# A decoder layer on one core: the value half of the last compressed sequence moves from the 256-key query tile to the last one

## The chip, the cores and the metric

The kernel runs on one core of a Trainium2 chip. The metric is the device time of one execution in microseconds (us); less is better. Each number under "time" is a median of several runs of the same kernel. TensorE is called PE, VectorE DVE, ScalarE ACT, GpSimd POOL and SyncE SP; SP only issues transfers here.

## The reference

One step of a hybrid decoder layer is computed for two groups that share the weights: a prompt of 1024 tokens, and 8 sample sequences of 8 new tokens each behind 2048 past ones. The layer is a half feed-forward block, a combined projection, attention and a Mamba-2 mixer side by side, the projection w_out, and a second half feed-forward block. Every attention has a compressed branch. For the sample group its keys and values come from the cache: overlapping blocks of 32 past tokens go through a small two-layer network, for keys (K) and for values (V) with weights of their own.

```python
def compress(rows, pe, w1, w2):
    ...
    blk = jnp.concatenate([ch[:, :-1], ch[:, 1:]], axis=2) + pe[None, None, :, None, :]
    blk = blk.transpose(0, 1, 3, 2, 4).reshape(b, nc - 1, KV_HEADS, CMP_BLOCK * HEAD_DIM)
    return jax.nn.silu(blk @ w1) @ w2

def nsa_mixer(q, q_pos, full_cmp, full_sel, o_win, gates, prm, slopes, sel_qb):
    kc = compress(full_cmp[:, :, 0], prm['cmp_pe_k'], prm['cmp_w1_k'], prm['cmp_w2_k'])
    vc = compress(full_cmp[:, :, 1], prm['cmp_pe_v'], prm['cmp_w1_v'], prm['cmp_w2_v'])
    o_cmp, p_cmp = cmp_attention(q, q_pos, kc, vc, slopes)
    idx = select_blocks(p_cmp, q_pos, n_sel_blocks)
    o_sel = sel_attention(q, q_pos, idx, full_sel[:, :, 0], full_sel[:, :, 1], slopes, sel_qb)
    return g[:, :, 0] * o_cmp + g[:, :, 1] * o_sel + g[:, :, 2] * o_win
```

The kernel returns the outputs of both groups and their new cache rows and states.

## The kernel before

The program is one long list of instructions in which a scheduler fixes the order on each engine when the kernel is built, after the dependencies and the order in which the code emits them. Matrix products in float32 are made of three matmuls on a high and a low part (names that end in h and l, or hi and lo).

**Prompt attention.** A loop runs over eight query tiles of 128 queries, in the order `KN["qt"] = (2, 7, 6, 5, 4, 3, 1, 0)`. Tile 1, the seventh, sees 256 keys; tile 0, the eighth and last, sees 128. For each tile and head PE computes scores `s` (lines 1808, 1810, 1813), VectorE their maximum `mx` (1818), ScalarE the exponentials `pb` (1824), which are scaled by the row sums; PE transposes them (`pT`, 1846) and multiplies by the values (`o`, 1855). The eight exponentials of each of the two branches make 16 per tile.

**Compression of the samples.** It is emitted as work beside the query tiles: the list `KN["cs"]` says how many of the eight sequences are emitted ahead of each tile. `compress_sample(b)` gathers the cached rows `chk` of one sequence (POOL, 1689), and does the K half and then the V half. A half has four steps `pairs(kv, jj)`: two copies `chp` (267), four transposes `cT` on PE (1712), and the split into `th` (ScalarE) and `tl` (VectorE, 1717). Each step feeds 12 matmuls `cA` with the weights `w1h` and `w1l` (1733 to 1735). Behind four steps come the hidden layer `cxh` (1410 to 1414), two matmuls `c` (1740 for K, 1743 for V), and the copy to `kcTs` or `vcs`. `pairs` runs one step ahead of its matmuls, over the border from K to V too. The last sequence, number 7, is emitted ahead of the 256-key tile.

**What comes next.** After the query tiles the space of the compression (the weights `w1h` among it) is given up, and `sample_attention()` uses it. It loads `big` (SP, 1951), a table of constants, masks and selector rows; the window rows `schk` (SP, 2052); the rows of the selected blocks, `schk` as well, by gathers on POOL (2048). SP also brings rows `xT` (1892) and pieces `raw` of w_out (1900). PE transposes the rows (`kT_ps`, 2064), computes gates (`a_ps<-gates,big`, 1985) and scores of the compressed keys (`a_ps<-kcTs,QS`, 1994), from which a chain of short instructions on VectorE and ScalarE (1987 to 2004, ending in `pcg`) makes the probabilities that choose the blocks (2006 onward). The matmuls `wout` (250 to 252) of the projection fill PE between the parts of that stage.

Of the kernel before, what the change touches and what calls it, by code (L numbers as in the profile page):

```python
# [18 lines left out]
P = 128  # L19
# [15 lines left out]
PAST = 2048  # L35
AHEAD = 5
EARLY = {(0, 0): (0, 128), (1, 0): (640,), (0, 1): (), (1, 1): (768,)}
KN = {'Bt': 'a', 'cb': 'a', 'de': 'vv', 'ea': 'pp', 'st': 'p', 'hT': 'v', 'xm': 'p', 'yz': 'v', 'kT': 'aa', 'sPT': 'v', 'ce': 'v', 'cm': 'v', 'pcT': 'v', 'msk': 'a', 'osb': 'av', 'q': 'sspss', 'pb': ['apppaapp', 'apppappp', 'apppappp', 'apvpappp', 'apppapvp', 'appvappp', 'vpvvvpvv', 'pvvvvvvv'], 'pc': 'p', 'ob': 'aa', 'QA': 'aapv', 'QB': 'pv', 'chp': 'ap', 'th': 'aa', 'qt': (2, 7, 6, 5, 4, 3, 1, 0), 'cs': [3, 0, 2, 1, 1, 0, 1, 0]}
SLOPES = [2.0 ** -(h + 1) for h in range(NH)]


# [39 lines left out]
def hybrid_step(ctx: ExitStack, tc: tile.TileContext, *aps):  # L81
    nc = tc.nc
# [1591 lines left out]
    with pool("att", bufs=2) as K, pool("att_ps2", bufs=3, space=PSUM) as PS2, \  # L1674
# [27 lines left out]
        def compress_sample(b):  # L1702
            chk = gather(b) if b else first_chk
            def pairs(kv, jj):
                chp = CK.tile([P, 2, 2, 2, 64], F32, name="chp", bufs=1)
                for g in range(2):
                    copy(KN["chp"][g], chp[:, :, g], chk[:, 4 * jj:4 * jj + 4, kv, g, :].rearrange(
                        "p (j r) d -> p j r d", r=2))
                q = b1("cT")
                for u in range(2):  # L1710
                    for g in range(2):
                        nc.tensor.transpose(q[:, P * (2 * u + g):P * (2 * u + g) + P],
                                            chp[:, u, g].rearrange("p r d -> p (r d)"), ident)
                sv = q.rearrange("p (u c) -> p u c", u=2)
                th, tl = tpad[jj % 2]
                copy(KN["th"][jj % 2], th[:, :, :256], sv)
                nc.vector.tensor_tensor(tl[:, :, :256], sv, f32(th[:, :, :256]), op=OP.subtract)

            steps = [(kv, jj) for kv in range(2) for jj in range(4)]
            pairs(*steps[0])  # L1720
            for kv in range(2):
                ab = PSC.tile([P, 2, P], F32, name="cA")
                for jj in range(4):
                    if (kv, jj) != steps[-1]:
                        pairs(*steps[4 * kv + jj + 1])
                    th, tl = tpad[jj % 2]
                    for u in range(2):
                        j = 2 * jj + u
                        for z in range(2):
                            wh, wl = w1h[:, kv, 8 * z + j], w1l[:, kv, 8 * z + j]  # L1730
                            first = j == 0 and z == 0
                            mh, ml = (x[:, u, z:z + 256].rearrange("p (g c) -> p g c", g=2) for x in (th, tl))
                            nc.tensor.matmul(ab, wh, mh, start=first, stop=False, skip_group_check=True)  # L1733
                            nc.tensor.matmul(ab, wl, mh, start=False, stop=False, skip_group_check=True)
                            nc.tensor.matmul(ab, wh, ml, start=False, stop=(j == 7 and z == 1), skip_group_check=True)
                hs = cmp_hidden(CK, ab[:, :, :127], None, kv, 127)
                q = b1("c2")
                for g in range(2):
                    if kv == 0:
                        nc.tensor.matmul(q[64 * g:64 * g + 64, :127], w2[:, 0], hs[:, g, :127],  # L1740
                                         start=True, stop=True)
                    else:
                        nc.tensor.matmul(q[:127, 64 * g:64 * g + 64], hs[:, g, :127], w2[:, 1],
                                         start=True, stop=True)
                if kv == 0:
                    nc.vector.tensor_copy(kcTs[:, b, :127], q[:, :127])
                else:
                    nc.vector.tensor_copy(vcs[:127, b, :], q[:127, :P])

        sequences = iter(range(8))  # L1750
        for qi, qt in enumerate(KN["qt"]):
            tq = slice(P * qt, P * qt + P)
            for _ in range(KN["cs"][qi]):
                compress_sample(next(sequences))
            QBq = QBs[2 * (qi % 2):2 * (qi % 2) + 2]
            lo_, up_ = slice(0, 64), slice(64, 128)
            QAs = QA0
# [27 lines left out]
            for g in range(2):  # L1785
                PT = {}
                for br in range(2):
# [6 lines left out]
                    for hh_ in range(4):  # L1794
# [26 lines left out]
                                nc.vector.tensor_reduce(mx[:, 1 + i:2 + i], parts[i][0], axis=AX.X, op=OP.max)  # L1821
                            nc.vector.tensor_reduce(mx[:, 0:1], mx[:, 1:3], axis=AX.X, op=OP.max, negate=True)  # L1822
                        for i, (s, st, pn) in enumerate(parts):
                            nc.scalar.activation(pb[:, st:st + pn], s, AF.Exp, bias=mx[:, 0:1],  # L1824
                                                 accum_out=part[:, hh_, i:i + 1])
                    total = part[:, :, 0]
                    if ns == 2:
                        total = sm[:, 1 + br, hs_]
# [35 lines left out]
                copy(KN["ob"][1], ob[up_], Ov[up_, :, 1])  # L1864
                nc.vector.tensor_tensor(qT[lo_, 2 * g:2 * g + 2, tq], Ov[lo_, :, 0], ob[lo_], op=OP.add)
                nc.vector.tensor_tensor(qT[up_, 2 * g:2 * g + 2, tq], Ov[lo_, :, 1], ob[up_], op=OP.add)
    Ds.close()
    KVs.close()

# [663 lines left out]
```

## Time and profile before

| | before |
|---|---|
| median of 3 runs | 2470.27 us (2468.21 to 2471.36) |
| the profiled execution, own time | 2475.45 us |
| its span, first to last instruction | 2473.8 us |
| its mean granted PE clock | 0.987 |
| PE busy | 2408.8 us, 97% |
| DVE, ACT, POOL busy | 1744.7, 1131.2, 418.3 us |

A stretch's busy time on an engine is the time in which the engine worked on an instruction. The granted clock is a share of the full 2.4 GHz. The times of rows count from the first instruction of the profiled execution.

### The profile page before, as it was taken

What the parts mean: (1) busy time and instruction counts of PE and PEld (TensorE: products, weight loads), DVE (VectorE), ACT (ScalarE), POOL (GpSimd) and SP (SyncE); (2) the same over time, 40 slices, a digit from 0 to 9 for tenths busy, and PEclk for the clock granted to TensorE, in tenths of its full rate; (3) what the DMA queues carried; (4) which work ended last, traced back from release to release, by engine and by line L of the source; (5) the groups of instructions that cost most, each with busy time, mean ns of one, the idle gap of its engine ahead of it and who ended that gap; (6) DMA issues with size and microseconds to landing.
All of it is one profiled execution on the core that took longest, in us unless ns stands there. A gap on an engine that the chain in (4) does not pass through costs nothing.

```text
span 2473.8 us, 48193 instructions
## 1 busy us (share of the span) xinstructions
PE 2408.8 (97%) x19026; PEld 2222.8 (90%) x19026; DVE 1744.7 (71%) x3673; ACT 1131.2 (46%) x2501; POOL 418.3 (17%) x533
## 2 busy tenths in 40 slices
PE   7999999999999999999999999999999999999998
PEld 6999999999999998997667766677899999999998
DVE  6777776677778855655656666777967676768776
ACT  7544444441133254425666675444545454543113
POOL 0000000011134343333434343111000000001110
PEclk9999999999999999999999998999999999999999
DMA  4334343598652333423110104476235353559654
GB/s 162 134 133 160 130 164 129 175 338 306 230 190 84 126 116 102 119 69 127 40 64 35 69 35 148 130 250 213 89 123 171 120 174 120 174 213 370 238 209 153
DMA packets 230446, 379.07 MB, mean 153 GB/s; under 512 B 18509, under 2 KB 147705, under 8 KB 228812
## 3 DMA queue, kind: packets, MB, share of 16 engines
q1 hardware_dynamic: 210248, 318.02, 37.7%
q0 software_dynamic: 7600, 38.59, 4.5%
q10 hardware_dynamic: 12372, 19.38, 2.2%
q8 instruction: 150, 2.46, 0.4%
q14 instruction: 76, 0.62, 0.1%
HBM read 255.66 MB, written 124.40 MB: 154 GB/s over the span
## 4 chain that ended last, share of the span: by engine, by line
PE 86%; DVE 6%; DMA 4%; ACT 3%; issue 1%; POOL 0%; ACTq 0%; DVEq 0%; POOLq 0%
PE dq L634 6%; PE gY L367 6%; PE dq L633 6%; PE dq L635 6%; PE gY L368 6%; PE gY L366 6%; PE gX L367 5%; PE gX L366 5%; PE gX L368 5%; PE o L1855 3%; PE pT L1846 3%; PE s L1808 1%; PE xbc L250 1%; PE xbc L251 1%; PE xbc L252 1%; PE cA L1733 1%
## 5 line engine op out<-in xcount | busy, mean ns | idle before, releaser
L634 PE MATMUL dq<-db,da 128*128 128x256 f32 (+1 forms) x1232 | 353.2, 288 | 0.3 <-DVE da L270 0.3
L635 PE MATMUL dq<-db,da 128*128 128x256 f32 (+1 forms) x1232 | 352.8, 288 | 0.0
L633 PE MATMUL dq<-db,da 128*128 128x256 f32 (+1 forms) x1232 | 349.8, 288 | 2.7 <-DVE Cc L386 2.2
L642 DVE TENSOR_TENSOR xT<-xT,dq 128x256 f32<-128x256 f32 (+1 forms) x456 | 186.9, 432 | 84.8 <-PE dq L635 83.2
L270 POOL TENSOR_TENSOR ds<-dw 128x512 f32<-128x512 f32 x22 | 29.5, 1341 | 1228.1 <-DVE wlo L270 508.0
L633 PEld LDWEIGHTS dq<-db,da 128*128 128x128 f32 x1232 | 230.5, 189 | 3.3 <-DVE Cc L386 2.5
L635 PEld LDWEIGHTS dq<-db,da 128*128 128x128 f32 x1232 | 232.8, 189 | 0.0
L634 PEld LDWEIGHTS dq<-db,da 128*128 128x128 f32 x1232 | 231.9, 188 | 0.6 <-DVE da L270 0.5
L267 ACT CAST whi<-ws 128x512 fp32r<-128x512 f32 x156 | 96.5, 623 | 205.9 <-PE gY L368 137.6
L270 DVE TENSOR_TENSOR wlo<-raw,whi 128x512 fp32r<-128x512 f32 x184 | 125.5, 687 | 83.9 <-ACT whi L267 83.5
L267 ACT CAST da<-ds 128x512 fp32r<-128x512 f32 x88 | 52.6, 623 | 234.7 <-PE dq L635 93.4
L267 ACT CAST whi<-raw 128x512 fp32r<-128x512 f32 x181 | 112.4, 626 | 72.0 <-PE g L414 19.5
L270 DVE TENSOR_TENSOR wlo<-ws,whi 128x512 fp32r<-128x512 f32 x156 | 106.7, 687 | 42.4 <-ACT whi L267 41.9
L1824 ACT ACTIVATE pb<-s,mx 128x256 f32<-128x256 f32 (+3 forms) x192 | 105.0, 552 | 59.7 <-DVE mx L1822 37.6
L1846 PEld LDWEIGHTS pT<-ident,pb 128*128 128x128 f32 x528 | 59.6, 143 | 45.8 <-issue 40.1
L1821 DVE TENSOR_REDUCE mx<-s 128x1 f32<-128x384 f32 (+2 forms) x128 | 66.6, 536 | 44.0 <-PE s L1813 34.1
L366 PE MATMUL gY<-B3h,whi 128*128 128x256 f32 (+1 forms) x320 | 91.5, 287 | 1.5 <-ACT whi L267 1.4
L366 PE MATMUL gX<-B6h,whi 128*128 128x256 f32 (+1 forms) x320 | 91.3, 286 | 0.9 <-ACT Cc L373 0.9
L367 PE MATMUL gX<-B6h,wlo 128*128 128x256 f32 (+1 forms) x320 | 91.4, 286 | 0.6 <-DVE wlo L270 0.6
L367 PE MATMUL gY<-B3h,wlo 128*128 128x256 f32 (+1 forms) x320 | 91.6, 287 | 0.2 <-DVE wlo L270 0.2
L277 POOL TENSOR_TENSOR pb<-pb,sm 128x640 f32<-128x640 f32 (+7 forms) x70 | 85.1, 1238 | 37.6 <-DVE sm L1831 34.0
L367 PE MATMUL gY<-B2h,wlo 128*128 128x256 f32 (+1 forms) x320 | 91.4, 286 | 0.0
(763 smaller groups left out, 8548.1 us busy)
## 6 DMA issues: line engine op xcount, KB each, us to landing
db<-GD SPq DMA_DIRECT2D x42, 1632.0 KB
GD<-Cc SPq DMA_DIRECT2D x154, 272.0 KB
GD<-his SPq DMA_DIRECT2D x84, 272.0 KB
raw<-in_ffn_wu_dram SPq DMA_DIRECT2D x22, 1024.0 KB
dw<-in_ffn_wd_dram SPq DMA_DIRECT2D x44, 512.0 KB
raw<-in_ffn_wg_dram SPq DMA_DIRECT2D x21, 1024.0 KB
GD<-hp SPq DMA_DIRECT2D x70, 272.0 KB
db<-GD SPq DMA_DIRECT2D x14, 1088.0 KB
```

Source lines behind the costliest of these rows:

```text
L267: return nc.scalar.copy(out, src) if eng == "a" else ENGINES[eng].tensor_copy(out, src)
L270: ENGINES[eng].tensor_tensor(out, x, y, op=op)
L277: nc.gpsimd.tensor_tensor(out, x, by.to_broadcast(list(x.shape)), op=OP.mult)
L366: nc.tensor.matmul(q, ah[:, k], b_, start=first, stop=False, skip_group_check=True)
L367: nc.tensor.matmul(q, al[:, k], b_, start=False, stop=False, skip_group_check=True)
L368: nc.tensor.matmul(q, ah[:, k], c_, start=False, stop=(k == 3), skip_group_check=True)
L633: nc.tensor.matmul(q, x, bh[:, u, o], start=first, stop=False, skip_group_check=True)
L634: nc.tensor.matmul(q, y, bh[:, u, o], start=False, stop=False, skip_group_check=True)
L635: nc.tensor.matmul(q, x, bl[:, u, o], start=False, stop=(u == np_ - 1), skip_group_check=True)
L642: nc.vector.tensor_tensor(x, x, q, op=OP.subtract if i == 4 else OP.add)
L1824: nc.scalar.activation(pb[:, st:st + pn], s, AF.Exp, bias=mx[:, 0:1], accum_out=part[:, hh_, i:i + 1])
L1846: nc.tensor.transpose(tq_[:kn, P * hh_:P * hh_ + P], src, ident)
```

## The change

The compression becomes a generator that stops after each half, and the counts in `KN["cs"]` are in halves. Ahead of the 256-key tile one half is drawn from it, the K half of sequence 7. The V half is emitted behind the last query tile. Its four groups of transposes each get a dependency on an exponential of that tile (numbers 0, 4, 8 and 12), which keeps the scheduler from putting them earlier. For sequence 7 the step ahead no longer crosses from K to V.

```diff
--- before.py
+++ after.py
@@ -35,7 +35,7 @@
 PAST = 2048
 AHEAD = 5
 EARLY = {(0, 0): (0, 128), (1, 0): (640,), (0, 1): (), (1, 1): (768,)}
-KN = {'Bt': 'a', 'cb': 'a', 'de': 'vv', 'ea': 'pp', 'st': 'p', 'hT': 'v', 'xm': 'p', 'yz': 'v', 'kT': 'aa', 'sPT': 'v', 'ce': 'v', 'cm': 'v', 'pcT': 'v', 'msk': 'a', 'osb': 'av', 'q': 'sspss', 'pb': ['apppaapp', 'apppappp', 'apppappp', 'apvpappp', 'apppapvp', 'appvappp', 'vpvvvpvv', 'pvvvvvvv'], 'pc': 'p', 'ob': 'aa', 'QA': 'aapv', 'QB': 'pv', 'chp': 'ap', 'th': 'aa', 'qt': (2, 7, 6, 5, 4, 3, 1, 0), 'cs': [3, 0, 2, 1, 1, 0, 1, 0]}
+KN = {'Bt': 'a', 'cb': 'a', 'de': 'vv', 'ea': 'pp', 'st': 'p', 'hT': 'v', 'xm': 'p', 'yz': 'v', 'kT': 'aa', 'sPT': 'v', 'ce': 'v', 'cm': 'v', 'pcT': 'v', 'msk': 'a', 'osb': 'av', 'q': 'sspss', 'pb': ['apppaapp', 'apppappp', 'apppappp', 'apvpappp', 'apppapvp', 'appvappp', 'vpvvvpvv', 'pvvvvvvv'], 'pc': 'p', 'ob': 'aa', 'QA': 'aapv', 'QB': 'pv', 'chp': 'ap', 'th': 'aa', 'qt': (2, 7, 6, 5, 4, 3, 1, 0), 'cs': [6, 0, 4, 2, 2, 0, 1, 0]}
 SLOPES = [2.0 ** -(h + 1) for h in range(NH)]
 
 
@@ -1709,19 +1709,25 @@
                 q = b1("cT")
                 for u in range(2):
                     for g in range(2):
-                        nc.tensor.transpose(q[:, P * (2 * u + g):P * (2 * u + g) + P],
-                                            chp[:, u, g].rearrange("p r d -> p (r d)"), ident)
+                        tr = nc.tensor.transpose(q[:, P * (2 * u + g):P * (2 * u + g) + P],
+                                                 chp[:, u, g].rearrange("p r d -> p (r d)"), ident)
+                        if b == 7 and kv:
+                            tc.add_manual_dep(tr.ins, held_by[jj], mybir.DependencyInfo(
+                                mybir.DependencyClass.Sync, mybir.DependencyReason.DATA), reason="order")
                 sv = q.rearrange("p (u c) -> p u c", u=2)
                 th, tl = tpad[jj % 2]
                 copy(KN["th"][jj % 2], th[:, :, :256], sv)
                 nc.vector.tensor_tensor(tl[:, :, :256], sv, f32(th[:, :, :256]), op=OP.subtract)
 
             steps = [(kv, jj) for kv in range(2) for jj in range(4)]
+            ahead = b < 7
             pairs(*steps[0])
             for kv in range(2):
                 ab = PSC.tile([P, 2, P], F32, name="cA")
                 for jj in range(4):
-                    if (kv, jj) != steps[-1]:
+                    if not ahead and kv and not jj:
+                        pairs(1, 0)
+                    if (kv, jj) != steps[-1] and (ahead or jj < 3):
                         pairs(*steps[4 * kv + jj + 1])
                     th, tl = tpad[jj % 2]
                     for u in range(2):
@@ -1746,12 +1752,14 @@
                     nc.vector.tensor_copy(kcTs[:, b, :127], q[:, :127])
                 else:
                     nc.vector.tensor_copy(vcs[:127, b, :], q[:127, :P])
-
-        sequences = iter(range(8))
+                yield
+
+        sequences = itertools.chain.from_iterable(compress_sample(b) for b in range(8))
+        exps = []
         for qi, qt in enumerate(KN["qt"]):
             tq = slice(P * qt, P * qt + P)
             for _ in range(KN["cs"][qi]):
-                compress_sample(next(sequences))
+                next(sequences)
             QBq = QBs[2 * (qi % 2):2 * (qi % 2) + 2]
             lo_, up_ = slice(0, 64), slice(64, 128)
             QAs = QA0
@@ -1821,8 +1829,10 @@
                                 nc.vector.tensor_reduce(mx[:, 1 + i:2 + i], parts[i][0], axis=AX.X, op=OP.max)
                             nc.vector.tensor_reduce(mx[:, 0:1], mx[:, 1:3], axis=AX.X, op=OP.max, negate=True)
                         for i, (s, st, pn) in enumerate(parts):
-                            nc.scalar.activation(pb[:, st:st + pn], s, AF.Exp, bias=mx[:, 0:1],
-                                                 accum_out=part[:, hh_, i:i + 1])
+                            ex = nc.scalar.activation(pb[:, st:st + pn], s, AF.Exp, bias=mx[:, 0:1],
+                                                      accum_out=part[:, hh_, i:i + 1])
+                            if qi == 7:
+                                exps.append(ex.ins.name)
                     total = part[:, :, 0]
                     if ns == 2:
                         total = sm[:, 1 + br, hs_]
@@ -1864,6 +1874,9 @@
                 copy(KN["ob"][1], ob[up_], Ov[up_, :, 1])
                 nc.vector.tensor_tensor(qT[lo_, 2 * g:2 * g + 2, tq], Ov[lo_, :, 0], ob[lo_], op=OP.add)
                 nc.vector.tensor_tensor(qT[up_, 2 * g:2 * g + 2, tq], Ov[lo_, :, 1], ob[up_], op=OP.add)
+        held_by = [exps[n] for n in (0, 4, 8, 12)]
+        for _ in sequences:
+            pass
     Ds.close()
     KVs.close()
 
```

PE, around the end of the last query tile and the start of the sample attention. `cA` and `c` are of the compression, `pT` and `o` of the query tile, `kT_ps`, `a_ps`, `s_ps` and `so` of the sample attention. Before:

```order
L1846 MATMUL pT<-ident,pc 64x128 x4
L1855 MATMUL o<-pt,VA 64x512 x2
L1855 MATMUL o<-pt,VAc 64x512
L1985 MATMUL a_ps<-gates,big 128x24
L2064 MATMUL kT_ps<-ident,schk 128x128 x8
L2096 LDWEIGHTS zrow
L2096 MATMUL so<-oneh,zrow 128x384
L1994 MATMUL a_ps<-kcTs,QS 64x127 x2
L2064 MATMUL kT_ps<-ident,schk 128x128 x4
L2071 MATMUL s_ps<-skT,QS 64x512 x2
L2064 MATMUL kT_ps<-ident,schk 128x128 x4
L250 MATMUL wout<-oh,whi 128x512 x2
```

After the change, from the last matmul `cA` of the V half:

```order
L1741 MATMUL cA<-tl_13758,w1h 128x256
L1865 MATMUL o<-pt,VA 64x512 x2
L1865 MATMUL o<-pt,VAc 64x512
L1749 MATMUL c_18662<-w_179,cxh 127x64 x2
L2077 MATMUL kT_ps<-ident,schk 128x128 x8
...
L1998 MATMUL a_ps<-gates,big 128x24
L2098 MATMUL s_ps<-ksTs,QS 64x64 x2
...
L2019 MATMUL a_ps<-spc,big 128x127
L2112 MATMUL sPT_ps<-ident,pcg 127x128
L2116 MATMUL so<-vcs,pcT 32x64 x4
L2135 MATMUL sPT_ps<-ident,S 128x128 x4
L250 MATMUL wout<-oh,whi 128x512 x2
```

The last `cA` of the V half now stands three matmuls `o` and two `c` ahead of the first transpose of sample rows; before, it stood in the 256-key tile. The steps of the choice (`a_ps`, `sPT_ps`, `so`) now stand ahead of the first `wout`.

POOL, over the same two tiles. `chp` are copies of the V half, `pb` and `pc` scalings of the query tiles, `schk` the gathers of the sample attention. Before:

```order
L267 COPY chp<-chk 128x2x128 x3
L277 TENSOR_TENSOR pb_18160<-pb_18160,sm 128x256
...
L277 TENSOR_TENSOR pb_18199<-pb_18199,sm 128x256
L2048 DMA schk<-in_cache_sel_dram,idx_9814 128x1024
L277 TENSOR_TENSOR pb_18284<-pb_18284,sm 128x256
L2048 DMA schk<-in_cache_sel_dram,idx_9814 128x1024 x3
```

After the change:

```order
L267 COPY chp<-chk 128x2x128
L277 TENSOR_TENSOR pb_18354<-pb_18354,sm 128x128
L270 TENSOR_TENSOR pc<-pc,sm 128x512
L267 COPY chp<-chk 128x2x128 x2
L277 TENSOR_TENSOR pb_18462<-pb_18462,sm 128x128
L2061 DMA schk<-in_cache_sel_dram,idx_9814 128x1024 x4
L1976 MEMSET QS 128x512
L1987 MEMSET zrow 32x128
L2061 DMA schk<-in_cache_sel_dram,idx_9814 128x1024 x28
```

The first four gathers stood among the scalings of the 256-key tile (row width 256); now they stand behind the last scaling of the last tile (width 128). On SP the order stays: window rows, `big`, `xT`, `raw`, only that two `raw` now stand between the second and the third `xT`.

## Rows read from the trace of the kernel before

**Rows 1.** The page: span, and busy time of each engine

```profile
span 2473.8 us, 48193 instructions
...
PE 2408.8 (97%) x19026; PEld 2222.8 (90%) x19026; DVE 1744.7 (71%) x3673; ACT 1131.2 (46%) x2501; POOL 418.3 (17%) x533
```

**Rows 2.** Table by stretch: start:end, us, busy (count) of engines, clock, DMA share, GB/s

```profile
core 0: us, PE busy (x) PEld busy (x) DVE busy (x) ACT busy (x) POOL busy (x), PEclk, DMA share, GB/s
1490.70:1518.40 27.70, 27.11 (x199) 20.31 (x197) 20.57 (x52) 17.13 (x50) 7.57 (x12) 1.00 0.09 30
1518.40:1533.60 15.20, 14.28 (x96) 9.16 (x95) 12.47 (x42) 10.10 (x37) 4.89 (x7) 1.00 1.02 400
1533.60:1547.90 14.30, 14.30 (x48) 7.50 (x48) 7.07 (x31) 5.39 (x19) 4.87 (x7) 0.52 0.59 200
1547.90:1555.50 7.60, 6.24 (x29) 3.31 (x28) 6.55 (x20) 6.50 (x14) 0.00 (x0) 0.68 0.33 100
```

**Rows 3.** Timeline of PE, last tile: start, us, engine, line, operation, [idle before]

```profile
1518.85 1.08 PE L1855 MATMUL o<-pt,VA 128*64 128x512 f32 x4
...
1538.08 1.98 PE L1855 MATMUL o<-pt,VA 128*64 128x512 f32 x4
```

**Rows 4.** Timeline of PE, V half; last, VectorE's subtraction grouped by line

```profile
1490.62 0.60 PE L1712 MATMUL cT<-ident,chp 128*128 128x128 f32 x4
...
1503.83 0.37 PE L1735 MATMUL cA<-tl,w1h 128*128 128x256 f32 x1
...
1504.98 0.28 PE L1735 MATMUL cA<-tl,w1h 128*128 128x256 f32 x1
...
1517.89 0.65 PE L1743 MATMUL c<-w,cxh 128*127 128x64 f32 x4 [0.59 <-DVE cxh L1414]
...
L1717 DVE TENSOR_TENSOR tl<-cT,th 128x512 fp32r<-128x512 f32 x4 | 2.7, 687 | 0.9 <-ACT th L267 0.9
```

**Rows 5.** Waits of SP's queue (total, times, longest); timelines of PE, SP, POOL

```profile
SPq L2052 <- PE cA L1735: 382.6, 1, 382.6
...
1514.59 0.28 PE L1735 MATMUL cA<-tl,w1h 128*128 128x256 f32 x1
...
1514.90 0.83 SPq L2052 DMA_DIRECT2D schk<-in_cache_win_dram  x2
...
1515.03 1.01 POOL L2048 DMA_INDIRECT schk<-in_cache_sel_dram,idx  x1 [1.55 <-PE cA L1735]
```

**Rows 6.** Transfers: per queue, 1516 to 1524.8, then to 1531.7; issues, last number us

```profile
q1 hardware_dynamic: 379, 2.76, 79.8%
q0 software_dynamic: 189, 0.71, 21.7%
...
q0 software_dynamic: 387, 1.39, 49.7%
q1 hardware_dynamic: 713, 1.27, 47.9%
...
schk<-in_cache_win_dram SPq DMA_DIRECT2D x2, 512.0 KB
schk<-in_cache_sel_dram,idx POOLq DMA_INDIRECT x1, 9.8
...
big<-saD SPq DMA_DIRECT2D x1, 2276.0 KB
xT<-xD SPq DMA_DIRECT2D x4, 512.0 KB
...
raw<-in_w_out_dram SPq DMA_DIRECT2D x3, 256.0 KB
```

**Rows 7.** Timelines of PE and VectorE, start of the sample attention

```profile
1551.12 0.69 PE L1994 MATMUL a_ps<-kcTs,QS 128*64 128x127 f32 x4 [0.36 <-DVE gr L1987]
...
1553.70 1.07 PE L2071 MATMUL s_ps<-skT,QS 128*64 128x512 f32 x2
...
1555.47 1.20 PE L250 MATMUL wout<-oh,whi 128*128 128x512 f32 x2
...
1556.39 0.28 DVE L2004 TENSOR_SCALAR pcg<-spc,grow 128x127 f32<-128x127 f32 x1
```

## The prediction

> **What bounds it now.** I read the first lines of the page, then the stretches around the change, then single rows of the engine whose idle time ends each stretch. The page says that PE is busy for 2408.8 of 2473.8 us [rows 1], so a gain must come from PE work, PE idle time or PE clock. The profiled execution took 2475.45 us, 5.2 above the median of the three runs (2470.27); I make the sum on the profiled one and carry the difference over to the median. About 0.2%, 4.9 us, is what a measurement of this kernel can tell from no change.
>
> The table of stretches [rows 2] is cut where the change acts: the query tile of 256 keys from the first transposes of the last V half (27.7 us), the last query tile in two pieces (15.2 and 14.3 us), and the way from its end to the first w_out matmul (7.6 us). In the first, PE is busy for 27.11 of 27.70 us. In the last tile PE is busy too, but the clock falls: 1.00 in the piece to 1533.6, 0.52 after it. The same four matmuls o take 1.08 us before the fall and 1.98 behind it [rows 3]. These are the levels 2.4 and 1.2 GHz. Ahead of the fall PE had been busy for 14.28 of 15.20 us [rows 2], so short idles came before it.
>
> **What moves, and its price in the tile it leaves.** The V half of the last sequence is 16 transposes cT, 48 matmuls cA and the small matmuls c. Four cT stand as one row of 0.60 us; ten cA start between 1503.83 and 1504.98, a pitch of 0.128; the c row takes 0.65 [rows 4]. By pitch that is 16 x 0.1 + 48 x 0.128 + 0.5 = about 8 us of PE. It leaves the 256-key tile, which then has 27.7 - 8 = 19.7 us if PE stays dense. VectorE was busy for 20.57 us there [rows 2] and gives up some 3.4 (four subtractions, 2.7 [rows 4], and about 0.7 for a product of the hidden layer and a copy, an estimate), so it has 17.1 us in 19.7: close enough that some idle is likely.
>
> **The tile it enters.** At the full clock the last tile costs 15.2 + 14.3 - 6.75 (half of the 13.5 us at half clock) - 1 (idle of the first piece) = 21.7 us; with the moved 8 us, 29.7, as long as it is now. If the cover keeps the clock up, the 8 us are paid for by the clock. Both tiles then take 19.7 + 29.7 = 49.4 us if PE never waits, against 57.2 now. At the share of the first piece of the last tile (14.28 of 15.20, 0.94) they take 52.6, which I use: the four ties make the transposes wait for exponentials, so matmuls cannot all be drawn forward. Bounds: 49.4 (dense) and 57.2 (the clock falls as now, the moved work adds as much as it left). The end of the attention moves from 1547.9 to about 1543.3: a gain of 4.6, between 0 and 7.8.
>
> The Trainium skill (TensorE: Matmul & The Clock Gate, Part 1) says that the throttled state is the default and that activity releases it; the fall behind a piece that was busy at 0.94 agrees with it. By that rule alone a tile filled with the moved work would get back all of the 6.75 us, and the two tiles would take 49.4 us; by the idle share of the row they take 52.6.
>
> **What the move takes along: the loads of the next stage.** This term decides. SP's first load of the sample attention (the window rows schk) waited 382.6 us for the last cA of the V half, which is the last reader of the space that it is written to; POOL's first gather of schk waited 1.55 us for the same matmul. It is the row at 1514.59; the two loads were issued at 1514.90 and 1515.03 [rows 5]. Behind them on SP stand `big`, the sample rows xT and w_out's first pieces; on POOL the other gathers. So the loads ran while the last tile had 33 us to go: in its first piece the DMA share is 1.02 at 400 GB/s [rows 2]. They cost nothing.
>
> In the changed order the last cA has only three matmuls o and two c behind it before the first sample transpose. The loads' wait is unchanged, so they now begin at X, the end of that cA, about 2 us (two rows of o at 1.08) before the attention's end: X = 1541.3. Everything that they brought is then waited for:
> - By 1524.8 the SP queue had moved 2.76 MB and POOL's 0.71; in the next 6.9 us 1.27 and 1.39 [rows 6]. The window rows and `big` are 2 x 512 + 2276 KB = 3.38 MB [rows 6]. That is 2.76 plus 0.62 at 1.27 / 6.9 MB per us: `big` lands at 1528.2, 13.6 us behind the last cA. The first gather took 9.8 us in this burst [rows 6]. So `big` is there at X + 13.6.
> - PE's matmul of gates and `big` cannot pass before that, and in the changed order what feeds the choice of blocks stands before w_out. That chain ran from 1551.12 (a_ps on PE) to the end of pcg on VectorE at 1556.67, 5.5 us [rows 7]. With two more transposes and so: X + 20.
> - w_out's first piece is behind two of the xT loads: 3.38 + 1.05 + 0.26 MB, 4.69 on SP (sizes in [rows 6]). 4.03 were through at X + 17.1, the rest takes 2 to 4 us: X + 19 to 21, and its cast and weights follow. Both paths give the first w_out matmul at about X + 21 = 1562.3.
>
> Before it came at 1555.47 [rows 7]. Some sample work now stands ahead of it that used to stand behind: another pair of s_ps (1.07 [rows 7]), a group of transposes and the small matmuls of the choice, together 2 to 3.5 us; I take 2.8. So w_out is really late by 1562.3 - 1555.5 - 2.8 = 4.0 us. PE has idled before it, so its clock is at half at first; the first two took 1.20 us [rows 7] before as well, at part clock; I add 0.9, between 0 and 2. What follows is the same number of matmuls, and the order on PE is the same again from about 1750 us on; 0, with 3 either way for where stalls fall in the w_out stage.
>
> Sum: 2475.45 + 4.0 + 0.9 = 2480.4 for the profiled execution (the 4.6 of the tiles stands in X already), or 2475.2 carried to the median: about 0.2% slower. The gain in the tiles is real and more than eaten by a wait of about 13 us for loads that used to lie under the last tile. The changed ties themselves cost PE nothing that is not in the 0.94.
>
> **A rule on the queues.** In 1516 to 1524.8 the SP queue moved 2.76 of 3.47 MB, in the next piece 1.27 of 2.66 [rows 6]: SP got four fifths until the gathers were well under way, then half. The Trainium skill (DMA: Bandwidth & Descriptors, Queues, rings and completion order) says that each DMA engine goes round robin between the queue rows, a packet at a time. Halves from the start would bring `big` only at X + 18 and the sum 4 us higher; the row speaks against it at the start and for it later.
>
> **Rivals.**
> 1. Faster: the tiles run dense and the loads come sooner. If SP keeps nearly the whole rate (3.38 MB at the 400 GB/s of [rows 2] is 8.5 us, plus 1.5 to start), `big` is there at X + 10 and the first w_out at X + 16.5; with 49.4 us for the tiles X = 1538.1, so 1554.6, less the 2.8 of work: 3.7 better than now, 2466.6, and 2460 to 2468 with the chain of the choice between 4 and 5.5 us. It decides where the first w_out stands less than 16 us behind the last cA (1555.5 + 2.8 - 0.9 - 1541.3). For it speaks that the clock is the one visible loss in the last tile, against it the 9.8 us of the first gather.
> 2. No change: tiles between 49.4 and 52.6, first w_out at X + 17 to 19, which gives 2468 to 2472. Nothing in the rows excludes it; the two terms are uncertain by 3 to 4 each.
> 3. Slower still: the clock falls anyway. In the 256-key tile VectorE, 17.1 of 19.7 us, may leave PE as idle as in the first piece of the last tile. If the half clock holds for 10 us there, 5 are lost, X = 1546.3, and the sum is 2480.2, up to 2487.
> 4. The halves of the queues rule from the start, as worked out just above: 2479 to 2480, at the near end of the slower range.
> 5. That the change does not do what it says: only if the scheduler had left the V half where it was; the order on PE shows that it did not.
>
> **How the numbers follow.** Forecast (2472 to 2479, the loads' loss a little more than the tiles' gain): 0.45. Rival 1 (2460 to 2468): 0.18. Rival 2 (2468 to 2472): 0.13. Rivals 3 and 4 (2479 to 2487): 0.24. Against 2470.27, faster by over 0.2% (below 2465.3) is most of rival 1, 0.14. Within 0.2% are the rest of it, rival 2 and a little under half of the forecast: 0.04 + 0.13 + 0.21 = 0.38. Slower (above 2475.2) are the rest of the forecast and rivals 3 and 4: 0.24 + 0.24 = 0.48. The range 2464 to 2485 leaves out the far ends of rivals 1 and 3, about 0.1 and 0.07.
>
> **What the profile after would show.** The clock at 1.00 through nearly the whole last tile, and the end of the attention 2 to 7 us earlier; SP's first sample load and POOL's first gather right behind the last cA as before, now 1 to 3 us ahead of the attention's end; DMA near 390 GB/s behind it, and PE idle by 10 us or more in that stretch, waiting for schk and `big`; first w_out 19 to 22 us behind the last cA. I would be wrong if the loads started before the last cA, if PE had other work in that gap, or if the w_out stage, where loads and casts also pace PE, gave the lost time back.

## The result, and the profile after

The changed kernel takes 2490.7 us (median of 6 runs, 2486.46 to 2501.83) against 2471.74 us for the kernel before (6 runs, 2468.21 to 2476.53): a ratio of 1.0079, with a 95% interval from 1.0064 to 1.0094. It is 19 us slower. The forecast was 2475.2 us, 5 slower, with a range that ended at 2485; the sign was right and the size was not. The profiled execution of after took 2494.02 us.

The page of after, beside [rows 1]: the span is 18.5 us longer and PE is busy for 5.1 us more, with the same number of matmuls.

```profile
span 2492.3 us, 48176 instructions
...
PE 2413.9 (97%) x19026; PEld 2226.1 (89%) x19026; DVE 1746.2 (70%) x3673; ACT 1130.6 (45%) x2501; POOL 418.6 (17%) x533
```

The table by stretch of after, cut at the same events as I cut all later runs: the last two query tiles (from the last score matmul `s_cmp` of the 256-key tile to the last `o`), the way from there to the first w_out matmul, the w_out stage (first to last w_out matmul), and what comes behind it.

```profile
core 0: us, PE busy (x) PEld busy (x) DVE busy (x) ACT busy (x) POOL busy (x), PEclk, DMA share, GB/s
1488.80:1542.00 53.20, 51.51 (x342) 34.71 (x341) 40.40 (x120) 33.02 (x105) 10.60 (x17) 1.00 0.02 5
1542.00:1565.30 23.30, 10.96 (x60) 5.67 (x59) 9.21 (x33) 7.71 (x16) 7.20 (x9) 0.72 1.03 403
1565.30:1768.00 202.70, 193.10 (x1747) 146.65 (x1748) 153.00 (x407) 91.85 (x204) 25.08 (x24) 0.96 0.63 198
1768.00:2481.90 713.90, 707.84 (x5685) 705.62 (x5683) 522.45 (x997) 287.59 (x592) 29.11 (x22) 1.00 0.51 177
```

The same table of before, for the two stretches that [rows 2] doesn't have in this cut:

```profile
1488.80:1547.90 59.10, 57.59 (x348) 37.83 (x346) 40.80 (x123) 33.08 (x105) 17.34 (x25) 0.88 0.45 165
...
1555.50:1753.30 197.80, 189.84 (x1775) 145.39 (x1774) 153.76 (x419) 93.46 (x206) 24.68 (x24) 0.98 0.63 198
```

Read stretch by stretch: the tiles are 5.9 us shorter, the clock stays at 1.00 in them, and the DMA share falls from 0.45 to 0.02. The way to w_out grows from 7.6 us [rows 2] to 23.3, with DMA at 403 GB/s and PE busy for less than half of it. The w_out stage is 4.9 us longer, though it has 28 matmuls fewer. Behind it 3.8 us more are spent than before's 710.1.

The timeline of PE in after, from the last `cA` to the first w_out matmul:

```profile
1539.68 0.28 PE L1741 MATMUL cA<-tl,w1h 128*128 128x256 f32 x1
...
1541.01 1.07 PE L1865 MATMUL o<-pt,VAc 64*64 64x512 f32 x2
...
1551.61 1.08 PE L2077 MATMUL kT_ps<-ident,schk 128*128 128x128 f32 x4 [5.01 <-DMA schk<-in_cache_sel_dram,idx]
...
1555.58 0.40 PE L1998 MATMUL a_ps<-gates,big 64*128 64x24 f32 x2
...
1560.31 0.66 PE L2135 MATMUL sPT_ps<-ident,S 128*128 128x128 f32 x4
...
1565.28 1.50 PE L250 MATMUL wout<-oh,whi 128*128 128x512 f32 x2 [4.31 <-ACT whi L267]
```

The waits of SP's queue, and the timelines of SP, POOL and ScalarE in after:

```profile
SPq L2065 <- PE cA L1741: 406.3, 1, 406.3
```

```profile
1539.99 0.83 SPq L2065 DMA_DIRECT2D schk<-in_cache_win_dram  x2
...
1543.73 11.41 SPq L1913 DMA_DIRECT2D raw<-in_w_out_dram  x2
...
1540.12 1.01 POOL L2061 DMA_INDIRECT schk<-in_cache_sel_dram,idx  x1 [7.57 <-PE cA L1741]
...
1549.95 0.94 POOL L2061 DMA_INDIRECT schk<-in_cache_sel_dram,idx  x1 [0.30 <-issue]
...
1564.60 1.32 ACT L267 CAST whi<-raw 128x512 fp32r<-128x512 f32 x2 [5.57 <-DMA raw<-in_w_out_dram]
```

Both queues still wait for the last `cA`, as in [rows 5]. It now ends 2.0 us ahead of the attention's end instead of 33, so the loads begin there; POOL sends all eight gathers by 1550.9. The first w_out matmul waits for a cast of the first piece of w_out, and that cast for the transfer.

### The profile page after: what moved, and what is told of

Read it like the earlier page. It is cut to its first block, busy times and chain, and to the rows that moved or that the text cites. A ratio compares the mean times of both kernels' runs of the same rounds, so it can differ in the third digit from the quotient of the medians.

```text
span 2492.3 us, 48176 instructions
## 1 busy us (share of the span) xinstructions
PE 2413.9 (97%) x19026; PEld 2226.1 (89%) x19026; DVE 1746.2 (70%) x3673; ACT 1130.6 (45%) x2501; POOL 418.6 (17%) x533
## 4 chain that ended last, share of the span: by engine, by line
PE 86%; DVE 5%; DMA 5%; ACT 3%; issue 1%; POOL 0%; ACTq 0%; DVEq 0%; SPq 0%; POOLq 0%
PE gY L367 6%; PE gY L366 6%; PE gY L368 6%; PE dq L634 6%; PE dq L633 6%; PE dq L635 6%; PE gX L367 5%; PE gX L366 5%; PE gX L368 5%; PE o L1865 3%; PE pT L1856 3%; PE s L1816 1%; PE cA L1739 1%; PE xbc L250 1%; DMA raw<-in_w_out_dram 1%
## 5 line engine op out<-in xcount | busy, mean ns | idle before, releaser
L1829 DVE TENSOR_REDUCE mx<-s 128x1 f32<-128x384 f32 (+2 forms) x128 | 66.6, 536 | 43.2 <-PE s L1821 33.3
L367 PE MATMUL gX<-B7h,wlo 128*128 128x256 f32 (+1 forms) x320 | 91.4, 286 | 0.2 <-DVE wlo L270 0.2
```

The lines of the kernel that those rows point to most:

```text
L367: nc.tensor.matmul(q, al[:, k], b_, start=False, stop=False, skip_group_check=True)
```

## The experiments

Each ratio is against runs of the kernel before on the same chip. Theory A, that of the prediction: the loads that wait for the last `cA` begin too late. Theory B: the V half costs time where it now stands, by its ties and the order in the last tile. Theory C: the time goes in the other mix of sample work and w_out matmuls. Before and after themselves were profiled again too, to see how far a profile repeats. No version here beats the kernel before.

**Before again, twice, and after again.** No edit.

> The kernel before, unchanged, profiled once more: how far its stages differ from one execution to the next. If the 4 us that the changed kernel loses behind the last w_out matmul are chance, this profile differs by a few us from the first one there too.

> The kernel before, unchanged, a third profile. In the first the clock fell for 13.7 us in the last query tile, in the second it did not fall there at all. If the fall is chance, the two tiles take 54 to 59 us in this one, and the gain of the changed kernel in them is 1 to 5 us.

> The changed kernel once more, unchanged, profiled. The 23 us from the attention's end to w_out should repeat within 1 us if they are loads; the fall of the clock behind the w_out stage should not, if it is chance.

One run of each: 2473.75 and 2471.72 us for before, 2486.96 for after. The tables by stretch of before (second profile), before (third) and after (second):

```profile
1491.70:1545.90 54.20, 51.66 (x347) 34.76 (x345) 40.84 (x123) 32.76 (x105) 17.56 (x25) 1.00 0.42 156
1545.90:1553.50 7.60, 6.43 (x29) 3.32 (x28) 6.30 (x19) 5.90 (x13) 0.00 (x0) 0.66 0.79 274
1553.50:1753.20 199.70, 191.25 (x1776) 146.88 (x1775) 155.53 (x425) 94.02 (x208) 24.64 (x24) 0.97 0.62 196
```

```profile
1487.40:1542.90 55.50, 53.20 (x347) 36.05 (x346) 40.83 (x123) 32.95 (x105) 17.33 (x25) 0.97 0.43 157
```

```profile
1486.90:1540.20 53.30, 51.60 (x344) 34.80 (x342) 40.39 (x120) 33.07 (x105) 10.61 (x17) 1.00 0.02 5
1540.20:1563.50 23.30, 11.19 (x60) 5.85 (x59) 9.20 (x33) 7.73 (x17) 7.17 (x9) 0.69 1.03 401
1563.50:1764.30 200.80, 192.02 (x1747) 146.72 (x1748) 154.52 (x411) 91.84 (x204) 24.95 (x24) 0.96 0.63 199
```

The way to w_out repeats to 0.1 us. The tiles of before don't: 59.1, 54.2 and 55.5 us in three profiles of one program, and in the second the clock never fell in the last tile. Over two profiles of after and three of before the mean stages are 53.2, 23.3, 201.8, 712.2 and 56.3, 7.4, 198.4, 710.1 us: the sum differs by 18.3 us, about the 19.0 between the medians. Of it the way to w_out is 15.9; the tiles give back 3.0, and the w_out stage and what follows it add 3.4 and 2.1.

**Late loads alone.** The kernel before, V half in its old place; the first pair's loads, `big` and the first xT rows are tied to the last transposes `pT` of the last tile.

```diff
+    def late(d):
+        tc.add_manual_dep(d.ins, last_pT, mybir.DependencyInfo(
+            mybir.DependencyClass.Sync, mybir.DependencyReason.DATA), reason="late")
+        return d
...
-        nc.sync.dma_start(big, saD)
+        late(nc.sync.dma_start(big, saD))
```

> The kernel before, with the V half in its old place; only the first loads of the sample attention (big, the first window rows and gathers, the xT loads) wait for the last transposes of the last query tile. Theory A (the late loads are the loss): the tiles stay as before and PE idles about 12 us between the tile's end and the first w_out matmul, with a few more behind it: 2483 to 2495. Theory B (the loss comes from the V half inside the last tile, its ties, or the order that the scheduler then makes): 2470 to 2477.

2499.31 us, ratio 1.0101 (1.0080 to 1.0122). Its table by stretch:

```profile
1492.40:1547.70 55.30, 53.16 (x346) 35.73 (x345) 40.43 (x121) 32.90 (x105) 10.96 (x17) 0.97 0.03 6
1547.70:1575.40 27.70, 15.06 (x92) 8.13 (x91) 17.38 (x47) 8.89 (x19) 6.62 (x9) 0.63 0.96 369
1575.40:1776.90 201.50, 189.65 (x1711) 144.50 (x1711) 145.70 (x397) 91.09 (x201) 25.21 (x24) 0.96 0.60 194
```

The V half stands in its old place here, and the loads begin at 1545.5. The way to w_out is 27.7 us and the w_out stage is as long as after's. So late loads can cost as much as the whole change without a moved V half, as A says. Its time lies above A's range (2483 to 2495) and above after's. It is no exact copy: PE did 92 matmuls on the way and not 60, so the 27.7 us are not the same waits.

**The V half in the last tile, loads early.** Two kernels: after without the ties (`untied`: the lines `if b == 7 and kv: tc.add_manual_dep(...)` are gone; the V half is still emitted behind the last tile and the scheduler puts it into the tile), and one that also draws the V half ahead of the last tile.

```diff
-'cs': [6, 0, 4, 2, 2, 0, 1, 0]
+'cs': [6, 0, 4, 2, 2, 0, 1, 1]
```

> The changed kernel without the four ties: the V half is still emitted behind the last query tile, but the scheduler draws it forward, so that its last cA stands about 85 matmuls, some 15 to 18 us, ahead of the tile's end. Theory A: the loads start that much earlier, most of the 12 us of idle time goes, and the clock of the last tile stays up; 2465 to 2474. Theory B (the V half in the last tile costs by itself): 2480 or more.

> The V half is emitted ahead of the last query tile and without ties: the last cA stands 113 matmuls, some 20 us or more, ahead of the tile's end. Theory A: all loads lie under the last tile again, part of the tile's clock is kept; 2464 to 2471. Theory B: at or above the kernel before, 2472 to 2480.

Untied: 2471.93 us, ratio 0.9995 (0.9984 to 1.0007). Ahead of the last tile: 2472.89, 1.0002 (0.9988 to 1.0015). The table of untied:

```profile
1490.30:1543.60 53.30, 51.48 (x347) 34.76 (x345) 41.37 (x123) 33.19 (x105) 18.04 (x25) 1.00 0.33 127
1543.60:1554.10 10.50, 9.11 (x43) 5.48 (x43) 7.54 (x28) 6.21 (x14) 0.00 (x0) 0.67 0.99 359
1554.10:1748.50 194.40, 189.09 (x1758) 142.84 (x1759) 154.05 (x410) 93.23 (x207) 25.25 (x24) 0.98 0.62 201
```

The tiles are as short as after's (53.3) with the V half in them; behind them the way is 3 us longer than before's mean and the w_out stage 4 us shorter. Since the time is that of before, B is out as a cost of its place; what the ties cost goes with the time of the last `cA`. The kernel that draws the V half ahead of the last tile missed A's range and came out in B's, but no slower than before; its tiles took 56.1 us at a clock of 0.94, so little of the gain in clock that A hoped for shows.

**Ties to exponentials 0, 1, 2, 3.** In after, so that the last `cA` stands in the middle of the last tile.

```diff
-        held_by = [exps[n] for n in (0, 4, 8, 12)]
+        held_by = [exps[n] for n in (0, 1, 2, 3)]
```

> The changed kernel with the ties on exponentials 0 to 3 of the last tile in place of 0, 4, 8 and 12: the last cA stands 32 matmuls ahead of the tile's last o in place of 3, some 5 to 6 us earlier. Theory A: the loads start 4 to 5 us earlier and the time falls by about as much, 2484 to 2488. Theory B: no difference, 2488 to 2494.

2483.23 us, 1.0044 (1.0029 to 1.0060). With the others it makes a row of doses, read from the tables by stretch and the timelines of PE:

| kernel | start of the last `cA` ahead of the attention's end, us | way to w_out, us | ratio |
|---|---|---|---|
| before | 33.3 | 7.6 | 1 |
| ahead of the last tile | 25.4 | 7.0 | 1.0002 |
| untied | 18.4 | 10.5 | 0.9995 |
| ties 0 to 3 | 12.4 | 18.2 | 1.0044 |
| after | 2.3 | 23.3 | 1.0079 |

At a lead of 25.4 us the way is as short as before's, and at 18.4 it is 3 us longer without a cost in the total; below that, way and time grow as the lead shrinks. Each way is read from one profile. That of ties 0 to 3 is of its slowest run (2494.92 us), and its tiles took 57.5 us, 4.2 of them idle on PE.

**Which transfer is last.** In after, the last four gathers of the first pair are held until w_out's first piece has landed.

```diff
+                    if not pr and k > 2:
+                        tc.add_manual_dep(d.ins, raw_load[0], mybir.DependencyInfo(
+                            mybir.DependencyClass.Sync, mybir.DependencyReason.DATA), reason="behind raw")
```

> The changed kernel; of the eight gathers that POOL issues up front the last four wait for w_out's first piece to land. In the changed kernel's trace all eight run beside that piece, which landed 25 us behind the last cA. Theory A with the second four gathers as the part that was missing in the sum: the piece lands 4 us earlier, and the time falls by 2 to 4 us, 2486 to 2489. Otherwise: the gathers are missed later, and the time stays at 2490 or rises.

2481.34 us, 1.0039 (1.0024 to 1.0054). POOL and PE, then the table by stretch:

```profile
1539.45 0.28 PE L1741 MATMUL cA<-tl,w1h 128*128 128x256 f32 x1
...
1559.41 0.96 POOL L2064 DMA_INDIRECT schk<-in_cache_sel_dram,idx  x1 [13.60 <-DMA raw<-in_w_out_dram]
...
1560.77 0.81 PE L250 MATMUL wout<-oh,whi 128*128 128x512 f32 x2
```

```profile
1541.80:1560.80 19.00, 11.77 (x60) 6.35 (x59) 9.27 (x33) 7.91 (x17) 4.49 (x7) 0.64 1.04 400
1560.80:1754.30 193.50, 188.96 (x1748) 143.11 (x1747) 153.37 (x407) 91.18 (x204) 27.56 (x27) 0.98 0.67 216
```

The piece lands 19.7 us behind the end of the last `cA` instead of 24.6, and w_out starts 21.0 behind it instead of 25.3. The way is 4.3 us shorter, the w_out stage 7 to 9 (against after's two profiles): against the kernel before, half of the loss is back. The same edit where the loads are early, in untied and in before:

> The V half emitted behind the last tile without ties, and the last four of the first eight gathers behind w_out's first piece. If holding those gathers back is what made the w_out stage short in the changed kernel with that edit (193.5 us against 202.7 and 200.8), the stage is 190 to 195 here too and the time 2464 to 2470. If the stage's length comes from the scheduler's order alone, it is anywhere from 193 to 203, and the time 2468 to 2480.

> The kernel before, with only that edit on the gathers; its loads lie under the last tile anyway. If the held gathers shorten the w_out stage, it falls from 198 to about 193 and the time to 2465 to 2468. If they only helped because the loads were late there, no change: 2470 to 2474.

2472.56 us, 1.0001 (0.9990 to 1.0013), and 2472.24 us, 1.0001 (0.9990 to 1.0011); the w_out stage is 195.6 and 199.8 us. So the hold gives nothing by itself in that stage; it pays only where the gathers stand in w_out's way.

**`big` ahead of the window rows.** The emission order of the loads, in after, in untied, and in after with the gathers held.

```diff
-        nc.sync.dma_start(big, saD)
+        load_big = nc.sync.dma_start(big, saD)
...
+                    with tc.issue_after(load_big.ins):
```

> The changed kernel with one order added on SP: the window rows are issued behind big. big itself is written to space whose last readers are the copies chp, so it needs only those and no longer stands behind a load that waits for the last cA. Theory A (the wait for late loads is the loss): big comes some 6 to 8 us earlier and w_out's first piece has 2.3 MB less ahead of it; the first w_out matmul moves from 23 us to about 15 to 18 us behind the attention's end, and the time falls to 2480 to 2486. Theory C (the loss is in the way the scheduler mixes sample work and w_out, whatever the loads do): 2488 to 2494.

> The V half emitted behind the last tile without ties (last cA some 18 us ahead of the tile's end) and big ahead of the window rows on SP. Theory A: all loads lie under the last tile, the way from the tile's end to w_out falls by 2 to 3 us against the untied kernel; 2466 to 2470. Theory C: as the untied kernel, 2472.

> The changed kernel, V half and ties as they are, with both edits: big ahead of the window rows on SP, and the last four of the first eight gathers behind w_out's first piece. Theory A (late loads): big lands under the last tile, behind the last cA only window rows, four gathers and the first pieces are left, some 3.5 MB, so the first w_out matmul stands 10 to 14 us behind the attention's end and not 23; the time falls by 8 to 14 us to 2476 to 2483. Theory C (the mix of sample work and w_out decides): not below 2481, the value with the gathers alone.

2485.41 us, 1.0061 (1.0043 to 1.0078); 2480.84, 1.0038 (1.0025 to 1.0052); 2499.28, 1.0114 (1.0097 to 1.0131). PE in the first of them:

```profile
1537.59 0.28 PE L1741 MATMUL cA<-tl,w1h 128*128 128x256 f32 x1
...
1547.49 0.59 PE L1998 MATMUL a_ps<-gates,big 64*128 64x24 f32 x2 [6.65 <-DMA big<-saD]
...
1558.48 0.79 PE L250 MATMUL wout<-oh,whi 128*128 128x512 f32 x1 [4.42 <-ACT whi L267]
```

`big` is there 9.6 us behind the last `cA`, but w_out's first matmul still waits for the cast of its piece, until 20.6. I had thought that `big` could be loaded early; it couldn't (SP sent it at 1537.89, right behind the last `cA`), so this tested an order of loads and no earlier load.

In the order of the three kernels the way was 18.6, 11.9 and 15.8 us, and the w_out stage 203.0, 202.4 and 212.9. The scheduler also reordered the rest, so the edits don't stay in their place, and these runs tell little of their price. Only the first came out in A's range; the second was expected at 2466 to 2470 and the third at 2476 to 2483. The second matters for C: its loads are early (SP sent `big` at 1521.32, 18.8 us ahead of the attention's end), and still it takes 9 us more than untied, with a w_out stage that is 8.0 us longer. So that stage can be long with early loads too. How much of after's 3.4 us there comes from the late loads is not shown.

**The third pair's window rows early.** In after PE waits 0.92 and 1.44 us for these rows at 1648 to 1651, and SP sends them at 1641.98, behind 21 pieces of w_out. Here the pieces from the sixteenth on are issued behind them.

```diff
+        raw_n.append(m)
+        with tc.issue_after(wins[5].ins) if len(raw_n) > 15 else nullcontext():
```

> The changed kernel; on SP the window rows of the third pair of sequences are issued behind 15 pieces of w_out and not behind 21. In the changed kernel's trace PE waited 2.4 us for them in the w_out stage, and its clock fell right behind. If that is what the w_out stage lost: the stage falls by 3 to 6 us, the way to the first w_out stays at 23 us, total 2485 to 2488. If the rows only stand in for other late work: 2489 to 2493.

2490.28 us, 1.0076 (1.0060 to 1.0093): nothing is back. SP sent the rows at 1637.99, less than 5 us earlier counted from the first w_out matmul, since they now waited 24.6 us for a matmul `so`; PE's wait for them fell from 2.4 to 0.8 us. The stage keeps its length, and other waits have come in. One, of `wout` for `oh` from ScalarE, is 0.3 us in after and 3.7 here, in the list of waits:

```profile
PE wout L250 <- ACT oh L267: 3.7, 1, 3.7
```

```profile
1565.90:1768.70 202.80, 192.31 (x1746) 147.83 (x1747) 153.52 (x410) 92.22 (x204) 24.88 (x24) 0.95 0.62 197
```

So the waits for those rows alone are not what makes the stage of after longer.

## Why the prediction was wrong in size

Two steps of the sum failed. The load term put the first w_out matmul 21 us behind the last `cA`; it came 25.3 behind. And the w_out stage was to be 1.9 us shorter (a credit of 2.8 for sample work done ahead, 0.9 for the cold clock, 0 for what follows); it was 3.4 us longer on the mean of the profiles.

The working used the profiled execution, so I compare there. Forecast 2480.4, measured 2494.02 us, 13.6 more. By the stretches above: the first w_out matmul at 1565.3 instead of 1562.3 (+3.0: the way 4.3 too long, the tiles 1.3 shorter than forecast); the w_out stage 202.7 us instead of before's 197.8 - 2.8 + 0.9 = 195.9 (+6.8); behind it 713.9 instead of 710.1 (+3.8). Over the means of the profiles the stretches changed by -3.0 us (tiles, forecast -4.6), +15.9 (way, +11.4), +3.4 (w_out stage, -1.9) and +2.1 (behind it, 0): the stage and the way missed by most.

**The tiles: the time right, its reason partly.** Forecast was the attention's end at 1543.3 and the last `cA` at 1541.3; they are at 1542.0 and 1540.0. "A gain of 4.6, between 0 and 7.8" was 5.9 against the profile on record and 3.0 against the mean of three. The 6.75 us that the low clock was to cost, from [rows 2], is no fixed price: the tile stood at the low level for 13.7, 0 and 3.4 us in three profiles. Nor does the idle share of [rows 2] decide it: at this place PE was busy for 2.08 of 3.00 us in all three, and the clock fell at its end in the first, right behind it in the third, and stayed up in the second. The first and the second, in the columns of [rows 2]:

```profile
1531.00:1534.00 3.00, 2.08 (x17) 1.81 (x15) 2.37 (x11) 2.66 (x12) 1.04 (x1) 0.93 1.09 383
...
1534.00:1537.00 3.00, 2.08 (x18) 1.74 (x16) 2.46 (x12) 2.66 (x11) 1.04 (x1) 1.00 1.09 383
```

The Trainium skill (TensorE: Matmul & The Clock Gate, Part 1) says that the cold part at the start of one kernel varies from run to run; the three profiles show that a fall in the middle of one does too.

**The late loads: mechanism right, one term too small.** This is the step that carried the sign: SP's wait, POOL's wait, the DMA rate near 400 GB/s and the idle PE are as forecast, and the way to w_out, which they lengthen, is 15.9 of the 18.3 us. The choice of blocks was through when PE came to the next transposes, at 1560.3: X + 20, as forecast (X is the end of the last `cA`, 1540.0), in part by luck: PE waited for the first gathered rows until X + 11.6, no wait for `big` shows at the gates' matmul (X + 15.6, where X + 13.6 was forecast for `big`), and the chain behind it was shorter than forecast. But w_out's first piece, forecast for X + 19 to 21, came at X + 24.6, and the first w_out matmul at X + 25.3 instead of X + 21. I let SP keep the share that it had in [rows 6]. The queues of after moved, from 1540 to 1565:

```profile
q1 hardware_dynamic: 2848, 5.26, 57.0%
q0 software_dynamic: 1152, 4.19, 42.0%
...
schk<-in_cache_sel_dram,idx POOLq DMA_INDIRECT x8, 12.8
```

My sum of 4.69 MB on SP is about right, but 4.19 MB of gathers pass beside it. In the burst of before only 2.10 MB did ([rows 6]), four gathers; POOL sent the fifth 24 us behind the first, which stands at 1515.03 in [rows 5]:

```profile
1539.24 1.06 POOL L2048 DMA_INDIRECT schk<-in_cache_sel_dram,idx  x1 [0.16 <-issue]
```

After sends all eight within 11 us, and POOL's order after the change, known ahead of the prediction, has only two memsets between the fourth and the fifth. The hold of four gathers brings the first w_out matmul to X + 21.0, the forecast value, so the traffic of the second four is the missing term. The Trainium skill (DMA: Bandwidth & Descriptors, Issuing engines are not separate DMA queues) says that transfers of all engines run on the same 16 DMA engines and interleave; that run agrees, with 4.9 us for the piece. Halves from the start (rival 4) would be too early a share for POOL: in the first 13 us SP moved 3.48 MB and POOL 1.21.

**"What follows ... 0, with 3 either way", and the credit of 2.8.** This step failed. The w_out stage is longer, not shorter. Two profiles of after and three of before split it into matmul work at the full clock, time lost to the low clock and PE idle. Windows of after's second profile:

```profile
1563.50:1567.50 4.00, 4.00 (x9) 2.92 (x10) 4.00 (x7) 1.13 (x2) 0.00 (x0) 0.50 1.08 348
1567.50:1571.50 4.00, 4.00 (x20) 2.96 (x21) 3.94 (x7) 0.09 (x1) 0.00 (x0) 0.72 0.03 9
1571.50:1751.50 180.00, 171.44 (x1660) 128.61 (x1660) 134.33 (x365) 83.70 (x185) 24.95 (x24) 1.00 0.65 207
1751.50:1764.30 12.80, 12.57 (x66) 12.23 (x67) 12.25 (x35) 6.91 (x18) 0.00 (x0) 0.60 0.33 106
```

and of before's third:

```profile
1550.00:1554.00 4.00, 4.00 (x21) 3.19 (x19) 2.69 (x9) 1.53 (x3) 0.00 (x0) 0.97 0.57 167
1554.00:1738.00 184.00, 176.37 (x1710) 133.21 (x1709) 142.96 (x390) 86.38 (x190) 24.63 (x24) 1.00 0.65 207
1738.00:1747.80 9.80, 9.80 (x47) 9.68 (x47) 9.80 (x27) 5.99 (x15) 0.00 (x0) 0.50 0.11 38
```

A stretch at clock c loses (1 - c) of its length. That is 8.2 us here in after and 8.7 in its first profile, against 5.0, 4.4 and 6.0 in before's third, first and second: +3.3 on the mean. Idle is 8.8 and 9.6 against 7.6, 8.0 and 8.5: +1.2. The remaining work is 1.2 us less. Together +3.3, the difference between the mean stages but for rounding. So of the 2.8 us credited for sample work done ahead, 1.2 are there; and the 0.9 for the cold clock was too small: behind the long wait w_out's first 8 us lost 2.0 (first profile of after) and 3.1 us (above) to the low level, before's first 4 us 1.0, 0.8 and 0.1, so 1.9 more on the mean. But a long wait does not always leave the clock low: in the kernel with late loads alone w_out's first 4 us, behind a way of 27.7 us, ran at 1.00, as they did with the gathers held, and its stage was 201.5 us all the same:

```profile
1575.40:1579.40 4.00, 4.00 (x20) 3.31 (x20) 1.50 (x8) 1.40 (x3) 0.00 (x0) 1.00 0.86 274
```

Part of the rest lies in the middle, though in one profile of after only: the first, from 1649.3, behind the waits for the window rows:

```profile
1649.30:1653.30 4.00, 2.62 (x40) 1.97 (x40) 1.11 (x6) 1.91 (x7) 0.59 (x1) 0.73 1.02 340
```

Why the stage differs by 20 us among kernels whose work in it is about the same (193.5 to 212.9 us; the work 181 to 189 by the same split) stays open. The clock goes with it, 0.98 in the shortest and 0.94 in the longest, and so does PE's idle time, 4.5 and 13.4 us, but whether the clock is a cause or follows the waits isn't told apart; moving the window rows or holding the gathers alone did not settle it.

**Behind the last w_out.** 3.8 us of the gap to the forecast need not be the change's: over the profiles of all kernels this stretch took 708.5 to 715.0 us, before's own 708.5 to 711.8, and after's second took 710.6.

**The rivals.** Rival 1, faster, needed the first w_out matmul before X + 16, and rival 2, no change, at X + 17 to 19; it came at X + 25.3. Rival 3, the clock falling anyway in the tiles, didn't occur (1.00 there); in after it was low behind the wait instead. Rival 5 is out: the V half stands in the last tile. "If the w_out stage gave the lost time back" was my named doubt; it took more.

## What to carry to other kernels

When an instruction moves, ask which loads wait for it as the last reader of their space: the time between it and the end of the work that covers them is what hides them. Here 25 us of it hid them as well as before's 33, 18 nearly so, and 2.3 were left. Price such a burst by all bytes of all queues that start with it, not by the queue that you watch, nor by a share read where fewer of them ran. Profile the kernel before more than once before you count a low clock as a gain, and look at the clock behind each new wait: it cost 2 to 3 us in after, and nothing in the kernel with late loads alone.

## What was not expected of the hardware

The same program at the same place fell to the low clock for 13.7, 0 and 3.4 us in three profiles, with tiles of 59.1, 54.2 and 55.5 us, behind the same 0.92 us of idle PE. A gather of POOL took a median of 12.8 us from issue to landing in the burst of after, where 9.45 MB passed in 25 us.
